# Attention scores of three row blocks in one stretch, with the smaller blocks' exponentials a step later, and two delayed steps in the SSD groups

## The chip, the cores and the metric

The kernel runs on one core of one Trainium2 chip. The metric is the time of one execution on the device in microseconds (us), as the median of several runs.

The engines that matter here: TensorE (PE in the profile) multiplies matrices and transposes tiles; PEld is its loading of weights. VectorE (DVE) and ScalarE (ACT) do elementwise work, GpSimd (POOL) a few small powers and accumulating DMAs, SyncE (SP) issues most DMAs. Results of PE land in PSUM banks of 128 x 512 fp32, of which there are eight.

## The reference

One decoder layer for 512 tokens of width 1024, all in fp32. Cut to what matters:

```python
x = x + 0.5 * swiglu(rms_norm(x, norm_ffn1_w), ffn1_w_in, ffn1_w_out)
x = x + hybrid_mixer(rms_norm(x, norm_mix_w), ...)
x = x + memory_cross_attention(rms_norm(x, norm_cross_w), rms_norm(mem, norm_mem_w), ...)
x = x + 0.5 * swiglu(rms_norm(x, norm_ffn2_w), ffn2_w_in, ffn2_w_out)
return rms_norm(x, norm_final_w)

# in hybrid_mixer: 16 SSD heads in 4 groups, and 8 heads of differential attention
logits = einsum('bqhcd,bkhcd->bhcqk', q_blk, k) * scale + bias     # c = 0, 1: two score maps
logits = where(rel <= 0, logits, -inf)                              # causal, row blocks of 128
p = softmax(logits)
w = p[:, :, 0] - lam * p[:, :, 1]
out = einsum('bhqk,bkhe->bqhe', w, v)
# each SSD group's output is gated, then normed over the group's 256 channels:
yg = yg * rsqrt(mean(yg * yg) + EPS)
```

## The kernel before

**Precision.** Nearly every matmul of weights is done three times, with both operands split into a high and a low part of type fp32r (`split_into`, lines 152 to 161: ACT copies the high part, DVE subtracts to get the low part). A projection of one 128 x 512 tile (`proj`, line 324) is 24 matmuls of 512 columns.

**Stages.** First FFN, then the mixer (attention projections, heads, SSD groups, output projections), cross-attention, second FFN. In the trace the attention heads lie between about 375 and 640 us, SSD groups 2 and 3 between about 680 and 800 us, and the second FFN starts at about 950 us.

**What sets the order.** The program is written out by an `Order` object (lines 57 to 98). It has one dense stream, of generators that are run one after the other (`od.add`, lines 1156 to 1173), and chains (`od.spawn`), each with a due time on a host clock `od.t`. Every matmul advances that clock by a rough estimate: `mm` (line 144) by (columns + 8) / 2400 for one matmul of type fp32r, that is 0.217 per 512 columns. When a chain is due it does one step; the number that it yields is the distance, on that clock and counted from the start of the step, to its next step. So a head's scores are written between the dense matmuls of the next head's projections, which yield every two matmuls.

What is written out is not yet the order on the chip. On PE, DVE and ACT a planner orders the instructions: it plays the program with estimated durations and takes, on each engine, the earliest written instruction whose operands and buffers are there by its own reckoning. `with behind(...)` (line 184) forbids it to take an instruction ahead of a given one. SP and POOL keep the written order. On the chip each engine then runs its instructions in the planned order and waits by semaphores.

**PSUM.** Two pools of four banks each: `acc` (line 130), for projections of the dense stream, and `aux` (line 133), for the chains. A tile gets a bank of its pool that is free.

**A head** (`head`, line 766) starts 3.4 (`W["h0"]`) after its keys are projected. It handles four row blocks, i = 3, 2, 1, 0, with 128 queries each and 128 (i + 1) keys. `scores` (line 770) takes two PSUM banks, one for each of the two score maps, and places the given blocks side by side in them. The contraction is over 64 rows, so that the maps' matmuls run in pairs on two halves of PE: per block three passes of one pair (high x high, high x low, low x high). Then, per block and map, DVE adds the bias and finds the minimum (line 787, output `ec` and `mn`), and ACT takes the exponential and its row sum (line 788). `combine` (line 791) joins the two maps on DVE (lines 796 to 799, the long one being `ec<-ec,rl,ec`), and `turn(j)` (line 802) transposes the j-th key block of row blocks j to 3 on PE into a bank (`pt`), from which ACT and DVE split weights `wt` for the product with the values.

The steps (lines 814 to 830), each 3.3 (`W["hs"]`) after the one before: scores of block 3; scores of block 2 and `combine(3)`; scores of blocks 1 and 0, `combine(2)` and `turn(3)`; `combine(1)`, `combine(0)` and `turn(2)`; then `turn(1)`, and `turn(0)` 2.0 later.

Head 0 runs beside `values(0)` (line 724), which holds all four `acc` banks; heads 1 to 6 run beside the projections of later heads, heads 3 and 7 partly beside the `pxbc` tiles of an SSD group. Those are read by a convolution (`conv`, line 894: one operation on ACT, three on DVE).

**An SSD group** (`group`, line 928) works on two tiles j = 0, 1. For each, ACT and DVE make decay matrices (lines 987 to 993), and after `W["gd"]` = 6.9 and an extra, PE does the products `pf` and `py` (lines 995 to 1002). After gating (lines 1016 to 1021) and a distance of 11.8 (`W["gq"]`, and 1.2 more for group 2), `sums_by_token` (line 379) sums the squares by token on PE (`nps`), copies them by DVE (`nsum`) and, 0.8 later, transposes them. `inv_rms_cols` (line 364) then takes DVE (`nv`) and a power on POOL (`ncol`), and `row_of` (line 371), after a distance of 1.5 + 1.1, spreads the result by four transpositions (`nrow`) over the partitions. DVE scales both tiles by it (line 1028) and they are split into `ysh` and `ysl`, the operands of the output projection `out_proj` (line 1128). Its first two tiles do their first six of eight inputs early and then wait for group 3's two.

Of the kernel before, what the change touches and what calls it, by code (L numbers as in the profile page):

```python
# [13 lines left out]
AF = mybir.ActivationFunctionType  # L14
ALU = mybir.AluOpType
AX = mybir.AxisListType

P = 128
T = 512
# [18 lines left out]
W = {"h0": 3.4, "hs": 3.3, "ht": 2.0, "hv": 2.08, "hp": 6.75}  # L38
# [62 lines left out]
def body(tc, a, dbg=None):  # L101
# [13 lines left out]
    def nm(s):  # L115
        uid[0] += 1
        return f"{s}_{uid[0]}"

    def s2(s, dt=F32, shape=(P, T)):
        if math.prod(shape[1:]) <= T // 2:  # L120
            return sp.tile(list(shape), dt, tag="s1", name=nm(s), bufs=NHALF)
        return sp.tile(list(shape), dt, tag="s2", name=nm(s))
# [4 lines left out]
    def small(s, n, bufs=None):  # L127
        return tiny.tile([P, n], F32, tag=s, name=nm(s), bufs=bufs)
# [4 lines left out]
    def aux(s, shape=(P, T)):  # L133
        return aux_p.tile(list(shape), F32, tag="aux", name=nm(s))
# [6 lines left out]
    V, S, G = nc.vector, nc.scalar, nc.gpsimd  # L141
    od = Order()

    def mm(out, w, x, start, stop, share=1.0):
        od.t += share * (1 if w.dtype == R32 else 4) * (x.free_size() + 8) / 2400
        newest_mm[:] = [nc.tensor.matmul(out, w, x, start=start, stop=stop).ins]  # L146
# [36 lines left out]
    @contextmanager  # L183
    def behind(ins):
        with ExitStack() as after:
            for i in ins:
                after.enter_context(tc.issue_after(i))
            yield
# [147 lines left out]
    for k in range(KT):  # L336
# [3 lines left out]
        w = s2("wa")  # L340
# [30 lines left out]
    def row_of(col, nb, apart):  # L371
        yield apart
        pr = aux("nrow", (P, nb * P))
        with behind(list(newest_mm)):
            for b in range(nb):
                transpose(pr[:, b * P : (b + 1) * P], col[:, b : b + 1].to_broadcast([P, P]))
        return pr
# [388 lines left out]
    def head(hd, q, kq, bias):  # L766
        es, w0, w1 = {}, {}, {}
        sm = [small("sm", 4) for _ in range(2)]

        def scores(*blocks):  # L770
            ps = [aux("ps") for _ in range(2)]
            parts, to = {}, 0
            for i in blocks:
                n = P * (i + 1)
                parts[i] = slice(to, to + n)
                to += n
                for j, (u, w) in enumerate(((0, 0), (0, 1), (1, 0))):
                    for c in range(2):
                        pc = slice(64 * c, 64 * c + 64)
                        mm(ps[c][:, parts[i]], q[u][pc, i * P : (i + 1) * P], kq[w][pc, :n], j == 0, j == 2)  # L780
            for i in blocks:
                n = P * (i + 1)
                es[i] = []
                for c in range(2):
                    ec = s2("ec", shape=(P, n))
                    mn = small("mn", 1, bufs=8)
                    V.tensor_tensor_reduce(out=ec[:, :n], in0=ps[c][:, parts[i]], in1=bias[:, T - n :], scale=0.125, scalar=3e38, op0=ALU.add, op1=ALU.min, accum_out=mn)  # L787
                    S.activation(ec[:, :n], ec[:, :n], AF.Exp, bias=mn, scale=-1.0, accum_out=sm[c][:, i : i + 1])  # L788
                    es[i].append(ec)

        def combine(i):

            n = P * (i + 1)
            e = es[i]
            rc = small("rc", 1)
            V.reciprocal(rc, sm[1][:, i : i + 1])
            rl = small("rl", 1)
            V.scalar_tensor_tensor(rl, sm[0][:, i : i + 1], nlam, rc, ALU.mult, ALU.mult)
            V.scalar_tensor_tensor(e[0][:, :n], e[1][:, :n], rl, e[0][:, :n], ALU.mult, ALU.add)
            e.pop()  # L800

        def turn(j):
            n = P * (4 - j)
            pt = aux("pt")
            for i in range(j, 4):
                transpose(pt[:, (i - j) * P : (i - j + 1) * P], es[i][0][:, j * P : (j + 1) * P])
            if n <= T // 2:
                both = s2("wt", R32, (P, 2, n))
                w0[j], w1[j] = both[:, 0], both[:, 1]
            else:  # L810
                w0[j], w1[j] = s2("wt", R32, (P, n)), s2("wt", R32, (P, n))
            split_into(w0[j], w1[j], pt[:, :n])

        scores(3)
        yield W["hs"]
        scores(2)
        combine(3)
        yield W["hs"]
        scores(1, 0)
        combine(2)  # L820
        turn(3)
        yield W["hs"]
        combine(1)
        combine(0)
        turn(2)
        yield W["hs"]
        turn(1)
        yield W["ht"]
        turn(0)
        yield W["hs"] + (0.8 if hd % 4 == 3 else 0.0)  # L830
        es.clear()
        while hd // 4 not in vs:
            yield 1.0
        v = vs[hd // 4]
        hs = slice((hd % 4) * P, (hd % 4 + 1) * P)
        po = aux("po")
        for n, (v_, w_) in enumerate(((0, w0), (1, w0), (0, w1))):
            for j in (0, 1, 2, 3) if n < 2 else (1, 2, 3, 0):
                mm(po[:, j * P :], v[j][v_][:, hs], w_[j], n + j == 0, n == 2 and j == 0)
        w0.clear()  # L840
        w1.clear()
        of = s2("of")
        S.activation(of, po, AF.Copy)
        yield W["hv"]
        pt = aux("ptk")
        for b in range(4):
            transpose(pt[:, b * P : (b + 1) * P], of[:, b * P : (b + 1) * P])
        ss = small("ss", 4)
        junk = s2("junk", shape=(P, P))
        for b in range(4):  # L850
            S.activation(junk, pt[:, b * P : (b + 1) * P], AF.Square, accum_out=ss[:, b : b + 1])
        ev = small("ev", 4)
        V.scalar_tensor_tensor(ev, sm[0], EPS, sm[0], ALU.mult, ALU.mult)
        V.scalar_tensor_tensor(ev, ss, 1.0 / P, ev, ALU.mult, ALU.add)
        rr = small("rr", 4)
        G.tensor_tensor(rr, ev, mhalf, ALU.pow)
        on = s2("on", shape=(P, 4, P))
        V.tensor_tensor(on, pt.rearrange("p (a b) -> p a b", b=P), rr[:, :, None].to_broadcast([P, 4, P]), ALU.mult)
        yield W["hp"]
        pt = aux("pot")  # L860
        for b in range(4):
            transpose(pt[:, b * P : (b + 1) * P], on[:, b])
        ya[hd] = split("ya", backwards(pt), wsub)
        dump(f"ya_{hd}", ya[hd][0])
# [63 lines left out]
    def group(g, bt, ct, xs, zs):  # L928
# [52 lines left out]
        for j in range(2):  # L981
            rs = rows_of.pop((g, j))
            py = aux("py")
            e2 = s2("e2")
            for hh in range(2):
                hd = 4 * g + 2 * j + hh
                pp = slice(64 * hh, 64 * hh + 64)
                r = rs[hh]
                S.activation(e2[pp], r[pp].rearrange("p a b -> p (a b)"), AF.Exp)
                for c in range(4):  # L990
                    S.activation(r[:, c], r[:, c], AF.Relu, bias=cum[:, c, hd : hd + 1], scale=-1.0)
                S.activation(r, r, AF.Exp, scale=-1.0)
                V.tensor_tensor(r, r, cbm, ALU.mult)
            yield W["gd"] + (W["gt"] if j == 0 else 0.5 if g == 2 else 0.0)
            pf = aux("pf")
            with behind(list(newest_mm)):
                for c in range(1, 4):
                    mm(pf[:, c * P : (c + 1) * P], st[c - 1][:, j * P : (j + 1) * P], ct[:, c * P : (c + 1) * P], True, True)
                for c in range(4):
                    for hh in (1, 0):  # L1000
                        pp = slice(64 * hh, 64 * hh + 64)
                        mm(py[pp, c * P : (c + 1) * P], xdt[c // 2][:, c % 2, (2 * j + hh) * 64 : (2 * j + hh + 1) * 64], rs[hh][:, c], True, True)
            if g < 3:
                decays(g + 1, j)
            dsk = dskh[:, 2 * g + j : 2 * g + j + 1]
            V.scalar_tensor_tensor(e2[:, P:], pf[:, P:], 0.5, e2[:, P:], ALU.mult, ALU.mult)
            y = s2("y")
            V.scalar_tensor_tensor(y, xs[j], dsk, py, ALU.mult, ALU.add)
            V.tensor_tensor(y[:, P:], y[:, P:], e2[:, P:], ALU.add)
            dump(f"y_{2*g+j}", y)  # L1010
            yz.append(y)
            yield W["gy"]
# [9 lines left out]
        yield W["gq"] + (1.2 if g == 2 else 0.0)  # L1022
        pn = yield from sums_by_token(sq[0], 4)
        rh = inv_rms_cols(pn, 4, 4.0 / (4 * 256), 4.0 * EPS)
        pr = yield from row_of(rh, 4, W["gn"] + 1.1)
        for j in range(2):
            n = 2 * g + j
            V.scalar_tensor_tensor(yz[j], yz[j], par[:, C_SSD + n : C_SSD + n + 1], pr, ALU.mult, ALU.mult)
# [643 lines left out]
```

## Time and profile before

| | us |
|---|---|
| median of 3 runs | 1289.73 (1289.62 to 1290.07) |
| the profiled execution's own time | 1289.51 |
| its span, first to last instruction | 1287.7 |
| PE busy in the span | 1275.9 |
| DVE busy | 969.3 |
| ACT busy | 708.2 |
| POOL busy | 111.6 |

How to read it: the span is the time in which any instruction ran; the profiled execution's time is 1.8 us longer. A timeline row gives the start in us, the length in us, engine, line of the helper that issued it (L146 for all matmuls by `mm`, L150 for transpositions), operation, output <- inputs, shapes and how many instructions were merged into the row; in brackets, the engine's idle time ahead of it and what ended that. The lengths of matmuls are modelled and overlap, so distances on PE are taken from start to start.

### The profile page before, as it was taken

The numbers are of one execution on the slowest core, as the hardware profiler recorded it, in microseconds if no ns is written. First come the engines' busy times: TensorE is split into PE (matmuls) and PEld (weight loads), VectorE is DVE, ScalarE is ACT, GpSimd is POOL, SyncE is SP. The second block draws the span as 40 slices with busy tenths as digits, with TensorE's granted clock in tenths as the row PEclk, the third lists the DMA queues.
The fourth block names the chain that finished last, engine by engine and source line by source line (L and its number), as shares of the span: only waits on it lengthen the run. The fifth ranks groups of instructions, "written<-read, shape, count | busy, mean of one in ns | idle before, by whom it ended". The sixth has DMA issues, their size and how long they took to land.

```text
span 1287.7 us, 20009 instructions
## 1 busy us (share of the span) xinstructions
PE 1275.9 (99%) x7673; PEld 1115.9 (87%) x7673; DVE 969.3 (75%) x1547; ACT 708.2 (55%) x1207; POOL 111.6 (9%) x135
## 2 busy tenths in 40 slices
PE   9999999999999999999999999999999999999996
PEld 7889998998988788877888878888899899989995
DVE  6988898788875786657768697546668878877886
ACT  7545564566654564446654566434475546545554
POOL 1001010002201011101102011020001000000000
PEclk9999999999999999999999999999999999999998
DMA  9468677789865436753376457593259776666662
GB/s 338 104 173 209 180 204 203 217 217 238 284 205 159 128 74 191 214 173 84 96 224 199 137 150 241 197 229 99 69 160 243 207 222 177 193 190 187 186 202 87
DMA packets 69695, 234.70 MB, mean 182 GB/s; under 512 B 8144, under 2 KB 9568, under 8 KB 69248
## 3 DMA queue, kind: packets, MB, share of 16 engines
q1 hardware_dynamic: 53504, 181.12, 41.9%
q0 software_dynamic: 13456, 45.67, 19.8%
q10 hardware_dynamic: 2640, 6.65, 1.6%
q8 instruction: 60, 0.98, 0.3%
q14 instruction: 35, 0.29, 0.1%
HBM read 231.25 MB, written 48.29 MB: 217 GB/s over the span
## 4 chain that ended last, share of the span: by engine, by line
PE 88%; issue 9%; ACT 1%; POOL 1%; DMA 1%; DVE 1%; POOLq 0%; DVEq 0%; ACTq 0%
PE qb L244 13%; PE pm L146 9%; PE qe L244 9%; PE qa L244 8%; PE ob L1328 7%; PE oa L1328 5%; PE oe L1328 4%; PE pk L146 3%; PE pv L146 3%; PE pq L146 3%; PE pcq L146 3%; PE pxbc L146 3%; PE pck L146 2%; PE pa L146 2%; PE pg L146 2%
## 5 line engine op out<-in xcount | busy, mean ns | idle before, releaser
L155 ACT ACTIVATE wh<-wr 128x1024 fp32r<-128x1024 f32 (+1 forms) x245 | 251.2, 1028 | 223.4 <-PE qe L244 31.0
L156 DVE TENSOR_TENSOR wl<-wr,wh 128x1024 fp32r<-128x1024 f32 (+1 forms) x245 | 290.0, 1186 | 74.6 <-ACT wh L155 60.2
L1308 ACT ACTIVATE wh<-wr 128x1024 fp32r<-128x1024 f32 (+1 forms) x74 | 72.8, 984 | 65.9 <-PE ob L1328 17.4
L1317 DVE TENSOR_TENSOR wl<-wr,wh 128x1024 fp32r<-128x1024 f32 (+1 forms) x74 | 82.7, 1126 | 12.9 <-ACT wh L1308 11.0
L788 ACT ACTIVATE ec<-ec,mn 128x512 f32<-128x512 f32 (+3 forms) x64 | 35.3, 554 | 21.9 <-DVE mn L787 21.9
L787 DVE CUSTOM_DVE_ANT_0 ec<-ps,bias 128x512 f32<-128x512 f32 (+3 forms) x64 | 28.1, 487 | 16.2 <-PE ps L146 16.1
L368 POOL TENSOR_TENSOR ncol<-nv,mhalf 128x4 f32<-128x4 f32 (+1 forms) x9 | 11.4, 1271 | 299.8 <-DVE nv L366 299.8
L901 DVE SCALAR_TENSOR_TENSOR conv<-pxbc,par,conv 128x511 f32<-128x511 f32 (+2 forms) x48 | 35.8, 745 | 1.9 <-ACT conv L897 1.3
L253 POOL DMA_DIRECT2D wr<-in_f2q x11 | 9.7, 879 | 306.1 <-DMA wr<-in_f2q 230.4
L146 PE MATMUL pxbc<-hnl,wh 128*128 128x512 f32 x128 | 35.6, 405 | 0.0
L146 PE MATMUL pxbc<-hnh,wh 128*128 128x512 f32 x128 | 34.7, 398 | 0.0
L146 PE MATMUL pxbc<-hnh,wl 128*128 128x512 f32 x128 | 32.5, 393 | 0.0
L456 DVE TENSOR_TENSOR gate<-qb,row 128x512 f32<-128x512 f32 x19 | 13.1, 692 | 20.3 <-PE qb L244 20.3
L146 PEld LDWEIGHTS pxbc<-hnh,wl 128*128 128x128 f32 x128 | 23.7, 188 | 5.2 <-issue 0.2
L146 PEld LDWEIGHTS pxbc<-hnl,wh 128*128 128x128 f32 x128 | 23.1, 188 | 4.9 <-issue 0.6
L146 PEld LDWEIGHTS pxbc<-hnh,wh 128*128 128x128 f32 x128 | 23.4, 189 | 4.6 <-issue 0.3
L253 POOL DMA_DIRECT2D wr<-in_f1q x16 | 14.0, 872 | 152.3 <-DVE wl L156 44.6
L457 ACT ACTIVATE gate<-gate 128x1024 f32<-128x1024 f32 x19 | 20.1, 1057 | 10.9 <-DVE gate L456 10.9
L146 PE MATMUL pv<-wh,hnh 128*128 128x512 f32 x64 | 25.4, 398 | 0.0
L146 PE MATMUL pv<-wh,hnl 128*128 128x512 f32 x64 | 25.1, 393 | 0.0
L155 ACT ACTIVATE s24h<-s 128x512 fp32r<-128x512 f32 x30 | 18.8, 627 | 9.0 <-DVE s L214 9.0
L155 ACT ACTIVATE s31h<-s 128x512 fp32r<-128x512 f32 x30 | 18.7, 624 | 7.3 <-DVE s L212 4.2
(472 smaller groups left out, 3506.3 us busy)
## 6 DMA issues: line engine op xcount, KB each, us to landing
wr<-in_f2q SPq DMA_DIRECT2D x44, 512.0 KB, 4.3
wr<-in_f1q SPq DMA_DIRECT2D x40, 512.0 KB, 4.7
wr<-in_f1b SPq DMA_DIRECT2D x23, 512.0 KB, 6.3
isum<-in_f2q SPq DMA_DIRECT2D x22, 512.0 KB, 6.2
wr<-isum SPq DMA_DIRECT2D x22, 512.0 KB, 3.5
wsum<-in_f2b SPq DMA_DIRECT2D x20, 512.0 KB, 5.6
wr<-wsum SPq DMA_DIRECT2D x20, 512.0 KB, 4.4
wr<-in_f1q POOLq DMA_DIRECT2D x16, 512.0 KB, 6.8
```

Source lines behind the costliest of these rows:

```text
L146: newest_mm[:] = [nc.tensor.matmul(out, w, x, start=start, stop=stop).ins]
L155: S.activation(hi, src, AF.Copy),
L156: V.tensor_tensor(lo, src, hi.bitcast(F32), ALU.subtract),
L244: newest_mm[:] = [nc.tensor.matmul(out, w_[:, wc], xs[kp][which][x_], start=first and j == 0 and f == 0 and kp == 0, stop=j == 2 and kp == ...
L253: last_sum[:] = [G.dma_start(raw, m, accum_op=ALU.add).ins]
L457: S.activation(gate, gate, AF.Silu)
L787: V.tensor_tensor_reduce(out=ec[:, :n], in0=ps[c][:, parts[i]], in1=bias[:, T - n :], scale=0.125, scalar=3e38, op0=ALU.add, op1=ALU.min, ...
L788: S.activation(ec[:, :n], ec[:, :n], AF.Exp, bias=mn, scale=-1.0, accum_out=sm[c][:, i : i + 1])
L901: V.scalar_tensor_tensor(y[:, d:], ps[:, : T - d], par[:, cw + j : cw + j + 1], y[:, d:], ALU.mult, ALU.add)
L1308: recent[:] = [S.activation(hi[:, i * n : (i + 1) * n], r, AF.Copy).ins for i, r in enumerate(raw)]
L1317: recent.append(V.tensor_tensor(lo[:, ns], r, hi[:, ns].bitcast(F32), ALU.subtract).ins)
L1328: newest_mm[:] = [nc.tensor.matmul(ps, a_[:, ts], b_[:, ws], start=first and k == 0 and j == 0, stop=k == n - 1 and j == 2, skip_group_che ...
```

## The change

Three things change.

- In heads 1 to 7, step 2 does the scores of blocks 2 and 0, side by side in two `aux` banks, and right behind them those of block 1 in two `acc` banks; then the minima of all three, the exponentials of block 2, and `combine(3)`. Step 3 has no scores left: it takes the exponentials of blocks 1 and 0, then `combine(2)` and `turn(3)` as before. Distances between steps stay. Head 0 keeps its order of scores (3, then 2, then 1 and 0); there only the exponentials of block 0 follow those of block 1 in a call of their own.
- In group 3 the products of tile j = 1 come 0.5 later, as they do in group 2 already.
- The row of a group's norm (`row_of`) comes at a distance of 1.5 + 1.4 in groups 0, 1 and 3 and of 1.5 + 4.6 in group 2, in place of 1.5 + 1.1.

```diff
-        def scores(*blocks):
-            ps = [aux("ps") for _ in range(2)]
-            parts, to = {}, 0
-            for i in blocks:
-                n = P * (i + 1)
-                parts[i] = slice(to, to + n)
-                to += n
-                for j, (u, w) in enumerate(((0, 0), (0, 1), (1, 0))):
-                    for c in range(2):
-                        pc = slice(64 * c, 64 * c + 64)
-                        mm(ps[c][:, parts[i]], q[u][pc, i * P : (i + 1) * P], kq[w][pc, :n], j == 0, j == 2)
-            for i in blocks:
+        def scores(*pairs):
+            parts = {}
+            for n_, blocks in enumerate(pairs):
+                ps, to = [(acc if n_ else aux)("ps") for _ in range(2)], 0
+                for i in blocks:
+                    n = P * (i + 1)
+                    parts[i] = [p_[:, to : to + n] for p_ in ps]
+                    to += n
+                    for j, (u, w) in enumerate(((0, 0), (0, 1), (1, 0))):
+                        for c in range(2):
+                            pc = slice(64 * c, 64 * c + 64)
+                            mm(parts[i][c], q[u][pc, i * P : (i + 1) * P], kq[w][pc, :n], j == 0, j == 2)
+            for i in parts:
                 n = P * (i + 1)
                 es[i] = []
                 for c in range(2):
                     ec = s2("ec", shape=(P, n))
                     mn = small("mn", 1, bufs=8)
-                    V.tensor_tensor_reduce(out=ec[:, :n], in0=ps[c][:, parts[i]], ..., accum_out=mn)
-                    S.activation(ec[:, :n], ec[:, :n], AF.Exp, bias=mn, scale=-1.0, accum_out=sm[c][:, i : i + 1])
-                    es[i].append(ec)
+                    V.tensor_tensor_reduce(out=ec[:, :n], in0=parts[i][c], ..., accum_out=mn)
+                    es[i].append((ec, mn))
+            exponentials(pairs[0][0])
+
+        def exponentials(*blocks):
+            for i in blocks:
+                for c, (ec, mn) in enumerate(es[i]):
+                    S.activation(ec, ec, AF.Exp, bias=mn, scale=-1.0, accum_out=sm[c][:, i : i + 1])
+                es[i] = [ec for ec, _ in es[i]]
...
-        scores(3)
+        scores((3,))
         yield W["hs"]
-        scores(2)
-        combine(3)
-        yield W["hs"]
-        scores(1, 0)
+        if hd:
+            scores((2, 0), (1,))
+            combine(3)
+            yield W["hs"]
+            exponentials(1, 0)
+        else:
+            scores((2,))
+            combine(3)
+            yield W["hs"]
+            scores((1, 0))
+            exponentials(0)
         combine(2)
         turn(3)
         yield W["hs"]
...
-            yield W["gd"] + (W["gt"] if j == 0 else 0.5 if g == 2 else 0.0)
+            yield W["gd"] + (W["gt"] if j == 0 else 0.5 if g > 1 else 0.0)
...
-        pr = yield from row_of(rh, 4, W["gn"] + 1.1)
+        pr = yield from row_of(rh, 4, W["gn"] + (1.4, 1.4, 4.6, 1.4)[g])
```

More of the change, by code (lines that the diff above doesn't have):

```diff
@@ L786, in scores @@
                     mn = small("mn", 1, bufs=8)
-                    V.tensor_tensor_reduce(out=ec[:, :n], in0=ps[c][:, parts[i]], in1=bias[:, T - n :], scale=0.125, scalar=3e38, op0=ALU.add, op1=ALU.min, accum_out=mn)
-                    S.activation(ec[:, :n], ec[:, :n], AF.Exp, bias=mn, scale=-1.0, accum_out=sm[c][:, i : i + 1])
-                    es[i].append(ec)
+                    V.tensor_tensor_reduce(out=ec[:, :n], in0=parts[i][c], in1=bias[:, T - n :], scale=0.125, scalar=3e38, op0=ALU.add, op1=ALU.min, accum_out=mn)
+                    es[i].append((ec, mn))
[5 more added lines that the diff above has]
+                es[i] = [ec for ec, _ in es[i]]
         def combine(i):
```

## The prediction

> **What bounds the kernel now.** I read the page's first part, then busy time by stage, then TensorE's waits, and last the order of instructions around the edits. The page first, then the windows (us, busy time of PE, weight loads, DVE, ACT and POOL with instruction counts, granted clock, DMA share, GB/s), then the waits of PE.
>
> ```profile
> span 1287.7 us, 20009 instructions
> PE 1275.9 (99%) x7673; PEld 1115.9 (87%) x7673; DVE 969.3 (75%) x1547; ACT 708.2 (55%) x1207; POOL 111.6 (9%) x135
> ...
> 375.00:660.00 285.00, 284.97 (x1498) 227.52 (x1497) 193.30 (x460) 152.57 (x375) 25.77 (x29) 1.00 0.51 142
> 660.00:830.00 170.00, 169.41 (x868) 137.81 (x867) 128.56 (x187) 92.72 (x159) 16.83 (x21) 1.00 0.62 188
> 830.00:1270.00 440.00, 440.00 (x2893) 403.27 (x2892) 323.12 (x447) 236.07 (x340) 25.43 (x30) 1.00 0.62 178
> ...
> PE nrow L150 <- POOL ncol L368: 0.5, 1, 0.5
> ```
>
> TensorE is the bound everywhere, at a granted clock of 1.00. The attention heads lie in the first window, the last two SSD groups in the second; behind them PE has not one free 10 ns until 1270. So a microsecond that PE saves in the first two windows reaches the end, and one that it loses does too. The busy time hides two things, since a matmul's modelled end reaches to the next start: slow starts at a change of shape, and short waits. Both must be read from start to start.
>
> **The stretch of scores that goes.** The order on PE in head 4, from its step 2 (block 2, 384 wide) to the first transposition of step 3 and on; the last two rows are a lone transposition among dense matmuls, elsewhere:
>
> ```profile
> 566.17 0.44 PE L146 MATMUL ps<-kh,qh 64*128 64x384 f32 x2
> ...
> 566.89 1.65 PE L146 MATMUL pk<-hnh,wh 128*128 128x512 f32 x6
> 568.38 1.52 PE L146 MATMUL pk<-hnl,wh 128*128 128x512 f32 x6
> 569.83 0.38 PE L146 MATMUL ps<-kh,qh 64*128 64x256 f32 x2
> 570.06 0.28 PE L146 MATMUL ps<-kl,qh 64*128 64x256 f32 x2
> 570.17 0.28 PE L146 MATMUL ps<-kh,ql 64*128 64x256 f32 x2
> ...
> 570.46 0.28 PE L146 MATMUL ps<-kh,ql 64*128 64x128 f32 x2
> 570.67 0.33 PE L150 MATMUL pt<-ident,ec 128*128 128x128 f32 x1
> 570.75 0.71 PE L146 MATMUL pk<-hnl,wh 128*128 128x512 f32 x2
> 571.30 2.00 PE L146 MATMUL pk<-hnh,wl 128*128 128x512 f32 x8
> 573.13 0.62 PE L146 MATMUL pq<-hnh,wh 128*128 128x512 f32 x2
> ...
> 790.73 0.27 PE L150 MATMUL nps<-ident,nsum 128*128 128x128 f32 x1
> 790.75 1.62 PE L146 MATMUL pm<-ysh,wl 128*128 128x512 f32 x6
> ```
>
> A dense 512-wide matmul takes 0.229 us (eight from 571.30 to 573.13). The six before the stretch take 1.45 (568.38 to 569.83) where 1.37 is due: 0.08 to enter. The first pair of 64-row matmuls takes 0.23, the next 0.11: 0.12 more. From the last pair to the transposition is 0.21, where a pair of this size takes no more than 0.11: 0.10 to leave. The transposition holds PE for 0.08 behind scores and for 0.02 among dense matmuls: 0.06. Together 0.36 per stretch, of which the last part is the least sure: **0.30 to 0.36**; I take 0.35. For heads 1 to 7 the stretch (1, 0) goes: the same 12 matmuls stand behind block 2's in one stretch, which was entered and left anyway. 7 x 0.35 = **2.45 us** (2.1 to 2.5). Head 0 keeps its three stretches; its four small exponentials only stand behind its four minima, at no price, since they feed combines two steps on.
>
> The Trainium skill, page "TensorEngine Tiling (Array Packing)", section "Key Properties", says that a change of tiling mode drains TensorE. Its one drain per change is here the 0.08 and the 0.10; by that alone the stretch would give 7 x 0.18 = 1.3 us and the forecast below would be 1288.1. The rows show the slow first pair too, and I go by them.
>
> **What moves on DVE.** The minima of blocks 0 and 1 come a step earlier. Head 4's DVE, then what matters of heads 5 (its block 2, its first transposition, its combine of block 3) and 6:
>
> ```profile
> 567.63 0.55 DVE L787 CUSTOM_DVE_ANT_0 ec<-ps,bias 128x384 f32<-128x384 f32 x1
> ...
> 569.03 0.75 DVE L799 SCALAR_TENSOR_TENSOR ec<-ec,rl,ec 128x512 f32<-128x512 f32 x1
> ...
> 570.77 0.42 DVE L787 CUSTOM_DVE_ANT_0 ec<-ps,bias 128x256 f32<-128x256 f32 x1
> ...
> 571.46 0.29 DVE L787 CUSTOM_DVE_ANT_0 ec<-ps,bias 128x128 f32<-128x128 f32 x1
> 571.67 0.29 DVE L787 CUSTOM_DVE_ANT_0 ec<-ps,bias 128x128 f32<-128x128 f32 x1
> ...
> 580.77 0.44 PE L146 MATMUL ps<-kh,qh 64*128 64x384 f32 x2
> 586.74 0.33 PE L150 MATMUL pt<-ident,ec 128*128 128x128 f32 x1
> 584.05 0.75 DVE L799 SCALAR_TENSOR_TENSOR ec<-ec,rl,ec 128x512 f32<-128x512 f32 x1
> ...
> 599.08 0.75 DVE L799 SCALAR_TENSOR_TENSOR ec<-ec,rl,ec 128x512 f32<-128x512 f32 x1
> 599.74 0.55 DVE L787 CUSTOM_DVE_ANT_0 ec<-ps,bias 128x384 f32<-128x384 f32 x1
> ```
>
> Four minima take 0.69 (570.77 to 571.46) and 0.42 (twice 0.21): 1.11 us of DVE. In heads 4 and 5 they now stand ahead of block 3's combine, which the first transposition reads (`turn(3)`). The combine would end at 569.78 + 1.11 = 570.89 in head 4 and at 584.80 + 1.11 = 585.91 in head 5. In head 6 the combine runs ahead of block 2's minima and is not touched.
>
> The transposition's written place moves forward too. A step's 3.3 is counted from the step's start, and its own scores count: (392 + 264 + 136) x 6 / 2400 = 1.98 for the three blocks, against 0.98 for one. That leaves 1.32, or four pairs of dense matmuls (0.43 each on that clock), where the rows have 12 matmuls. So it is written behind 0.72 (block 2, 566.17 to 566.89), 0.61 (blocks 1 and 0: 569.83 to 570.67, less the slow start and end) and 8 x 0.229 with 0.1 for leaving: 3.26 us behind 566.17, at **569.43**, 1.46 us before its combine ends. Head 5: 584.03, 1.88 before. Heads 1 and 2 go as 4 and 5 (the same pattern of queries and keys). Waiting in the written place would cost 2 x 1.46 + 2 x 1.88 = **6.7 us**, since every matmul of the dense stream is queued behind that transposition. Bounds: 0 to 6.7. I take 0.2, near the lower end, because the planner sets PE's order by readiness. The sums by token of group 2 show that:
>
> ```profile
> 749.85 0.43 PE L146 MATMUL nps<-ysq,ones 128*32 128x128 f32 x8
> ...
> 759.37 0.27 PE L150 MATMUL nps<-ident,nsum 128*128 128x128 f32 x1
> 759.40 1.17 PE L146 MATMUL pcv<-wh,hm 128*128 128x512 f32 x4
> 761.02 0.65 PE L150 MATMUL nrow<-ident,ncol 128*128 128x128 f32 x4 [0.45 <-POOL ncol L368]
> ...
> 780.52 1.07 PE L146 MATMUL pcv<-wh,hm 128*128 128x512 f32 x4
> 781.73 1.09 PE L146 MATMUL py<-th,xdt 128*64 128x128 f32 x16
> ```
>
> Their transposition is written 0.8 behind the sums and ran 9.5 us behind them, with dense matmuls in between: an operand that the planner reckons late costs PE nothing. What costs is its error.
>
> **Banks.** Block 1 takes two of the four accumulator banks. At step 2 of heads 1, 2, 4, 5 and 6 the other two hold the running projection and at most one that is being split, so I cost it at nothing. In head 3 a convolution still reads its bank while the third `pxbc` tile starts:
>
> ```profile
> 470.15 1.08 PE L146 MATMUL pxbc<-hnh,wh 128*128 128x512 f32 x4
> ...
> 473.08 0.74 DVE L901 SCALAR_TENSOR_TENSOR conv<-pxbc,par,conv 128x509 f32<-128x509 f32 x1
> ```
>
> If that tile had to take this very bank it would wait from 470.15 to 473.82: 3.7 us. Any freed bank will do, and the scores' two are read out with that step's minima: bounds 0 and 3.7, I take 0. The `ec` and `mn` tiles of blocks 1 and 0 are held a step longer, in pools where no row shows a wait: nothing.
>
> **The two delayed steps.** `nrow` of group 2 starts 1.62 us behind four matmuls that need 0.92 and 0.09 for following a transposition: **0.6 us** of waiting. It moves 3.5 of the host clock later, past its old place of 761.02; how far past depends on how far the planner had already put it off. Gain 0 to 0.6; I take 0.5. The other three groups' rows move by 0.3 from places without a wait: nothing. `py` of group 3 starts 1.21 behind four matmuls that need 0.92, with 0.08 for the change of shape: **0.2 us**, which the further 0.5 covers. But group 3's last row now comes 0.8 / 0.43 = two pairs of matmuls later, and the output projection waits for it:
>
> ```profile
> 793.57 0.60 PE L150 MATMUL nrow<-ident,ncol 128*128 128x128 f32 x4
> 797.21 0.61 PE L146 MATMUL pm<-ysl,wh 128*128 128x512 f32 x2
> ...
> 795.65 1.35 DVE L156 TENSOR_TENSOR ysl<-y,ysh 128x512 fp32r<-128x512 f32 x2
> ```
>
> The second low half is ready at 797.00 and used at 797.44: 0.44 to spare, against 4 x 0.229 = 0.92. Cost 0 to 0.5, less where the planner brings other matmuls forward; I take 0.1. The group's row and norm on DVE and ACT come later among the same work, and `ys` of group 2 isn't read before the output projection.
>
> **The sum.** -2.45 - 0.5 - 0.2 + 0.2 + 0.1 = -2.85 us against the profiled execution's 1289.51 (span 1287.7, 1.8 around it): 1286.66. That execution lies 0.22 below the median of 1289.73, so **1286.9**.
>
> **The rivals.**
> - *The planner puts the transposition back, but too little.* It was 0.6 early with `nrow` and 0.2 with `py`. At 0.4 in each of heads 1, 2, 4 and 5, 1.6 us come back in place of my 0.2: 1288.3. For: four chains with an operand later than the written place. Against: PE shows no such wait at any transposition of a head today.
> - *The written order holds* (the slower side). PE waits at the first transposition in heads 1, 2, 4, 5: 1289.73 - 3.15 + 6.7 = 1293.3. It decides from 5.7 us of waiting on (slower by 0.2%). Against: the 9.5 us above.
> - *The stretch doesn't stay whole*, dense matmuls coming between its parts for want of banks: only the two delays are left, 0.7: 1289.0.
> - *The delays give nothing*: `nrow` still waits 0.6 and the last row costs 0.5, `py` gains 0.2: 1289.73 - 2.45 + 0.2 + 0.5 - 0.2 = 1287.8.
> - *The convolution's bank is waited for*: 3.7 more: 1290.6.
>
> **How the numbers follow.** Forecast 0.52, with its own range 1286.3 to 1287.5; late transposition 0.20; stretch broken 0.09; idle delays 0.08; written order 0.08; bank 0.03. A measurement of this kernel can tell about 0.2%, 2.6 us, from no change: below 1287.15 is faster. Of the forecast 0.44 lies there, of the rest 0.01: faster 0.45. Slower is the written order and a worse bank, 0.09. The same: 0.46. The range must hold all but the last two cases and the lower end of the forecast: 1286.2 to 1289.2.
>
> **What the changed profile would show.** In heads 1 to 7 one `ps` stretch of 384, 128 and 256 wide pairs, some 1.33 us long, and no slow pair later. The four minima ahead of the 512-wide combine in heads 1, 2, 4 and 5. The first `pt` behind more than 8 dense matmuls there; if behind 8, a gap of 1.5 us from start to start. No POOL wait at `nrow`. The forecast is wrong if gaps over 0.3 us show ahead of `pt`, or ahead of the first `pm` that reads `ysl`, or if PE's saving is given back behind 830.

## The result: slightly slower, and the profile after

| | before | after |
|---|---|---|
| median of 12 runs, us | 1290.18 (1289.59 to 1291.35) | 1292.99 (1292.53 to 1294.14) |
| the profiled execution's own time | 1289.51 | 1292.89 |
| its span | 1287.7 | 1291.1 |

The ratio is 1.0022, with a 95% interval of 1.0014 to 1.0029: 2.8 us slower. The forecast was 1286.9 with a range of 1286.2 to 1289.2, so the time lies outside it, on the side that had been given 0.09. In the experiments below one execution of run 7 (1564.98 us) and one of run 10 (7222.68 us) stood far above the rest; the medians include them, the ratios don't.

The profile after begins so:

```profile
span 1291.1 us, 20020 instructions
...
PE 1275.2 (99%) x7673; PEld 1117.1 (87%) x7673; DVE 967.4 (75%) x1547; ACT 708.0 (55%) x1207; POOL 111.2 (9%) x135
```

The span grew by 3.4 us while PE, with the same 7673 matmuls, was busy 0.7 us less. What was added is time in which PE does nothing. The busy time by stage (window, its length, PE, weight loads, DVE, ACT, POOL, granted clock, DMA share, GB/s) says where:

```profile
375.00:660.00 285.00, 280.99 (x1487) 225.82 (x1486) 190.87 (x456) 150.02 (x366) 25.87 (x29) 1.00 0.52 141
660.00:830.00 170.00, 169.18 (x867) 137.64 (x866) 126.49 (x186) 94.63 (x166) 16.04 (x21) 1.00 0.66 190
830.00:1270.00 440.00, 440.00 (x2893) 403.40 (x2892) 323.17 (x444) 235.02 (x338) 25.44 (x30) 1.00 0.63 178
```

In the stage of the heads PE was busy for all but 0.03 of 285 us before; now 4.0 us are free. Behind 830 PE has nothing free, as before. PE's waits after (us in all, times, longest) name the instruction:

```profile
PE ptk L150 <- ACT of L857: 4.0, 4, 1.4
...
PE nrow L150 <- POOL ncol L368: 0.8, 1, 0.8
```

The first row did not exist before. `ptk` is the transposition of a head's attention output: the products with the values land in the bank `po`, ACT copies it to `of` (line 857, 843 before), and 2.08 of the host clock later (`W["hv"]`) PE transposes `of`. The four waits lie in heads 2, 3, 5 and 6, where the last products of one head fall between steps 2 and 3 of the next. Head 5's place on PE, in the timeline after:

```profile
586.78 0.85 PE L146 MATMUL po<-wt,vh 128*128 128x384 f32 x4
587.47 0.27 PE L150 MATMUL pt<-ident,ec 128*128 128x128 f32 x1
...
588.05 0.40 PE L146 MATMUL pk<-hnl,wh 128*128 128x512 f32 x1
589.40 0.66 PE L150 MATMUL ptk<-ident,of 128*128 128x128 f32 x4 [0.96 <-ACT of L857]
589.81 1.87 PE L146 MATMUL pk<-hnl,wh 128*128 128x512 f32 x7
```

From 588.05 to 589.40 one dense matmul is all that PE does, 1.35 us where 0.23 is due. The four places (heads 2, 3, 5 and 6) have 1.60, 0.97, 1.13 and 0.97 too much from start to start. Before, the scores of blocks 1 and 0 lay between the same `po` and `ptk`, and there was no wait:

```profile
585.12 0.85 PE L146 MATMUL po<-wt,vh 128*128 128x384 f32 x4
...
586.90 0.60 PE L150 MATMUL ptk<-ident,of 128*128 128x128 f32 x4
```

What ACT did meanwhile, after:

```profile
585.76 0.62 ACT L795 ACTIVATE ec<-ec,mn 128x384 f32<-128x384 f32 x1 [1.93 <-DVE mn L788]
...
587.00 0.51 ACT L795 ACTIVATE ec<-ec,mn 128x256 f32<-128x256 f32 x1
...
588.39 0.39 ACT L795 ACTIVATE ec<-ec,mn 128x128 f32<-128x128 f32 x1
...
588.77 0.57 ACT L857 ACTIVATE of<-po 128x512 f32<-128x512 f32 x1
```

And ACT in the same place before:

```profile
583.39 0.60 ACT L788 ACTIVATE ec<-ec,mn 128x384 f32<-128x384 f32 x1
...
586.01 0.60 ACT L843 ACTIVATE of<-po 128x512 f32<-128x512 f32 x1 [1.92 <-PE po L146]
587.31 0.51 ACT L788 ACTIVATE ec<-ec,mn 128x256 f32<-128x256 f32 x1 [0.70 <-DVE mn L787]
```

Before, ACT idled until `po` was there, copied it at once, and idled again until the minima of blocks 1 and 0 released their exponentials. After, those minima come right behind block 2's, so the exponentials are released ahead of the end of `po`, and the copy stands behind all six of the step (in heads 3 and 6 behind five of them). `po` ends at 587.63 by its row; `of` starts at 588.77, 1.14 us later. PE's next instruction is the transposition of it, and the whole dense stream is queued behind that. The Trainium skill, page "Perfetto Trace Analysis", section "Tensor Engine Instruction (MATMUL, LD_WEIGHTS)", says that the execution queues of ACT and DVE are strictly first in, first out; the trace agrees, since `of` had its operand 1.14 us before its turn came.

In heads 2 and 5 the six exponentials also start later: on DVE block 3's combine now goes ahead of block 2's minima (rows further down), so in head 5 the first exponential starts 3.12 us behind the first scores of step 2 (585.76 behind 582.64), where before it was 2.01 (582.78 behind 580.77). In head 6 that order on DVE is the old one, and the place has 0.97 too much all the same. What the later start adds in heads 2 and 5 was not tried by itself.

### The profile page after: what moved, and what is told of

Its sections match the earlier page's. It is cut to its first block, busy times and chain, and to the rows that moved or that the text cites. A ratio compares the mean times of both kernels' runs of the same rounds, so it can differ in the third digit from the quotient of the medians.

```text
span 1291.1 us, 20020 instructions
## 1 busy us (share of the span) xinstructions
PE 1275.2 (99%) x7673; PEld 1117.1 (87%) x7673; DVE 967.4 (75%) x1547; ACT 708.0 (55%) x1207; POOL 111.2 (9%) x135
## 4 chain that ended last, share of the span: by engine, by line
PE 85%; issue 9%; DVE 2%; ACT 2%; DMA 1%; POOL 1%; POOLq 0%; SPq 0%; DVEq 0%; ACTq 0%
PE qb L244 13%; PE pm L146 9%; PE qe L244 8%; PE qa L244 8%; PE ob L1342 7%; PE oa L1342 5%; PE oe L1342 4%; PE pv L146 3%; PE pcq L146 3%; PE pq L146 3%; PE pk L146 3%; PE pxbc L146 2%; PE pck L146 2%; PE pcv L146 2%; PE pa L146 2%
## 5 line engine op out<-in xcount | busy, mean ns | idle before, releaser
L155 ACT ACTIVATE wt<-pt 128x128 fp32r<-128x128 f32 (+3 forms) x32 | 13.8, 430 | 17.4 <-PE pt L150 17.2
```

What stands on the lines that cost most here:

```text
L155: S.activation(hi, src, AF.Copy),
```

## The experiments

The theory (A): the loss is `of` behind the exponentials, some 4.7 us of `ptk`'s waiting, and without it the change would gain. The rivals: the merged stretch itself costs (B); `ptk` is only written too close behind `po` (C); the cause is that the exponentials come "a step later" (D).

The kernel before had medians of 1290.14 to 1290.33 in the three sets of these runs, and work that no edit touches differs by more: the first `pdt` matmul on PE, behind the first FFN, starts between 374.92 and 376.89 in these profiles. So beside each ratio stands a length inside the profiled execution, from the first `pdt` matmul (374.92 before) to the first `pcq` matmul of the cross-attention (832.11 before). The heads and the SSD groups lie between the two. From that `pcq` to the end of the span all these profiles take 455.5 to 455.6, so what is lost or gained between the marks reaches the end, and a length of this size repeats to about 0.1. "Delays" are those of group 3's `py` and of the groups' rows, group 2's above all.

| kernel | `pdt` to `pcq` | against before | median | ratio to before (95%) |
|---|---|---|---|---|
| before | 457.19 | | | |
| after | 460.27 | +3.08 | 1292.99 | 1.0022 (1.0014 to 1.0029) |
| 1: exponentials behind `of` | 455.79 | -1.40 | 1289.23 | 0.9996 (0.9987 to 1.0005) |
| 2: exponentials at once | 460.01 | +2.82 | 1292.51 | 1.0019 (1.0010 to 1.0028) |
| 3: `ptk` later | 455.63 | -1.56 | 1288.17 | 0.9984 (0.9975 to 0.9993) |
| 4: heads' part only | 459.87 | +2.68 | 1293.00 | 1.0021 (1.0011 to 1.0030) |
| 5: delays only | 457.49 | +0.30 | 1290.79 | 1.0005 (0.9996 to 1.0014) |
| 6: after, row at 10.5 | 458.95 | +1.76 | 1292.20 | 1.0017 (1.0008 to 1.0026) |
| 7: 1 and 6 together | 454.55 | -2.64 | 1287.89 | 0.9980 (0.9971 to 0.9989) |
| 8: before, a stretch more per head | 460.15 | +2.96 | 1293.02 | 1.0023 (1.0013 to 1.0034) |
| 9: 3 and 6 together | 454.51 | -2.68 | 1287.44 | 0.9978 (0.9969 to 0.9986) |
| 10: before, delays with the row at 10.5 | 456.28 | -0.91 | 1289.51 | 0.9991 (0.9982 to 1.0000) |
| 11: heads' part only, exponentials behind `of` | 455.65 | -1.54 | 1288.56 | 0.9987 (0.9978 to 0.9996) |

**1. The exponentials of blocks 1 and 0 behind the copy.** The planner may not take them ahead of the newest `of`; nothing else changes.

```diff
+    newest_of = []
...
-            exponentials(1, 0)
+            with behind(list(newest_of)):
+                exponentials(1, 0)
...
-        S.activation(of, po, AF.Copy)
+        newest_of[:] = [S.activation(of, po, AF.Copy).ins]
```

> The changed kernel, with the exponentials of blocks 1 and 0 tied behind the last copy of a head's output (of) on ACT. Theory A (the new waits at ptk, 1.6, 1.0, 1.1 and 1.0 us in heads 2, 3, 5 and 6, together 4.7, come from of standing behind those exponentials in ACT's order): the waits go, one score stretch less stays, about 4.7 us below the changed kernel, 1288.3, and under the kernel before by 1.5 to 2.2. Theory B (the stretch itself costs: its banks or its early minima hold something up, and ptk is only where it shows): no more than 1 us is won, the gaps turn up at other instructions. Theory C (ptk is only written too close behind po, since the score stretch no longer lies between): waits of 0.3 us and more stay at ptk in all four heads.

It is 4.48 us shorter than the kernel after between the two marks, and PE's waits hold no `ptk` any more. The median fell less than expected: 1289.23 for 1288.3, not clearly below the kernel before. Head 5 on ACT:

```profile
585.06 0.60 ACT L859 ACTIVATE of<-po 128x512 f32<-128x512 f32 x1 [0.60 <-PE po L147]
585.56 0.50 ACT L796 ACTIVATE ec<-ec,mn 128x256 f32<-128x256 f32 x1
```

and on PE:

```profile
584.18 0.85 PE L147 MATMUL po<-wt,vh 128*128 128x384 f32 x4
...
585.44 0.40 PE L147 MATMUL pk<-hnl,wh 128*128 128x512 f32 x1
585.72 0.66 PE L151 MATMUL ptk<-ident,of 128*128 128x128 f32 x4
```

The transposition is in the same place (1.54 us behind the last `po` row's start, where the kernel after had 2.62) and has 0.05 too much in place of 1.13, since the copy goes first and four of the six exponentials follow it. With the stretch, the banks and the early minima all as in the kernel after, B falls; and C falls as the cause, since the place of `ptk` was not moved. That place is tight, though: the copy ends at 585.66 and `ptk` starts at 585.72.

**2. The exponentials at once.** All three blocks' exponentials are written in step 2.

```diff
-            exponentials(pairs[0][0])
+            exponentials(*parts)
...
-            exponentials(1, 0)
...
-            exponentials(0)
```

> The changed kernel, with the exponentials of all three blocks written in step 2, right behind their minima. Theory A: ACT takes them ahead of of as soon as the minima are there, whichever step writes them, so the four waits stay at about 4.7 us and the time at 1292.5 to 1293.3. Theory D (the exponentials' step later is what puts them in the way of of): the waits go and the time is 1288.3.

```profile
PE ptk L150 <- ACT of L855: 3.8, 4, 1.4
```

PE waits 3.8 us at `ptk`, four times, as in the kernel after (4.0), and the time is the same. The step that the change puts between minima and exponentials does nothing either way: the planner takes an exponential when its minimum is there, not where it is written. D falls. What makes the exponentials early is the minima, so the scores.

**3. `ptk` later.** The distance behind `po` grows from 2.08 to 3.88.

```diff
-W = {"h0": 3.4, "hs": 3.3, "ht": 2.0, "hv": 2.08, "hp": 6.75}
+W = {"h0": 3.4, "hs": 3.3, "ht": 2.0, "hv": 3.88, "hp": 6.75}
```

> The changed kernel, with ptk 1.8 later on the host clock (hv 3.88 in place of 2.08), ACT's order left alone. Theory A: of ends at most 1.4 us after ptk's old place, so the waits go as in e1: 1288.3, or 0.5 more if a head's last steps come late for the output projection behind heads 3 and 7. Theory B: no more than 1 us is won.

The copy still comes behind the exponentials, now without harm. On ACT and on PE, head 5:

```profile
586.40 0.39 ACT L795 ACTIVATE ec<-ec,mn 128x128 f32<-128x128 f32 x1
...
586.79 0.57 ACT L857 ACTIVATE of<-po 128x512 f32<-128x512 f32 x1
```

```profile
584.79 0.85 PE L146 MATMUL po<-wt,vh 128*128 128x384 f32 x4
...
586.06 1.99 PE L146 MATMUL pk<-hnl,wh 128*128 128x512 f32 x8
587.88 0.60 PE L150 MATMUL ptk<-ident,of 128*128 128x128 f32 x4
```

Eight matmuls of `pk<-hnl,wh` stand where one stood, and `of` is there when PE comes to it. So the late copy has a price only because the distance of 2.08 had been set for an early copy. Either end can be mended: the place of the copy or the place of its reader.

**4 and 5. The two parts alone.** Run 4 undoes the delays in the kernel after; run 5 makes only them in the kernel before.

```diff
-            yield W["gd"] + (W["gt"] if j == 0 else 0.5 if g > 1 else 0.0)
+            yield W["gd"] + (W["gt"] if j == 0 else 0.5 if g == 2 else 0.0)
...
-        pr = yield from row_of(rh, 4, W["gn"] + (1.4, 1.4, 4.6, 1.4)[g])
+        pr = yield from row_of(rh, 4, W["gn"] + 1.1)
```

> The changed kernel without its two delays in the SSD groups: heads alone. Theory A: the waits at ptk stay (4.7 us); nrow of group 2 waits 0.6 as before in place of 0.95, py of group 3 0.2 in place of 0.1: 0.1 to 0.3 us below the changed kernel, 1292.7. If the delays were the loss, the time would be 1290 or less.

> The kernel before with the two delays of the change alone (py of group 3 and the rows of the SSD groups). Prediction's step: 0.5 + 0.2 - 0.1 = 0.6 us below the kernel before. Theory A, from the kernel with the heads' part alone, where the waits were as before: the transposition of group 2's row (nrow) waits some 0.95 us from start to start in place of 0.61, py's excess goes from 0.30 to 0.21, and the time is 0.2 to 0.4 us ABOVE the kernel before, which this comparison calls no change. Attention heads as before: no wait of ptk on ACT.

The heads' part alone loses 2.68, the delays alone 0.30; together 2.98, against 3.08 for the whole. The delays were to gain 0.6 and cost a little. The row of group 2 in the kernel after:

```profile
762.57 0.27 PE L150 MATMUL nps<-ident,nsum 128*128 128x128 f32 x1
762.60 0.94 PE L146 MATMUL pm<-yah,wl 128*128 128x512 f32 x3
764.32 0.65 PE L150 MATMUL nrow<-ident,ncol 128*128 128x128 f32 x4 [0.79 <-POOL ncol L368]
```

The row still comes as early as its operand allows, now behind three matmuls in place of four, and waits 0.95 from start to start in place of 0.61. The planner had put it off beyond its written place already. An estimate from rows of before, with the host clock taken as us and the sums by token as run where they were written: they start at 749.85, the transposition is written 0.8 behind them and the row 2.6 behind that, at 753.3, while it ran at 761.02. With 3.5 more it is written at 756.8, still ahead of the planned place, and such a written place delays nothing. Why one matmul fewer was put in front isn't shown.

**6. The row later still.** Its distance in the kernel after is 10.5 in place of 4.6, behind the place that the planner chose (762.7 by the same estimate).

```diff
-        pr = yield from row_of(rh, 4, W["gn"] + (1.4, 1.4, 4.6, 1.4)[g])
+        pr = yield from row_of(rh, 4, W["gn"] + (1.4, 1.4, 10.5, 1.4)[g])
```

> The changed kernel with the delay of group 2's row 10.5 in place of 4.6, so that its written place lies behind the place where the planner put it, not ahead. Theory (the row was moved too little): the wait of nrow on POOL (0.95 us of start to start) is gone, the waits of ptk on ACT (some 4.7 us) stay, and the time is some 0.9 us below the changed kernel. Rival (the wait goes with the row, whatever its place, or the output projection waits for it later): nrow still waits, or a wait of the same size shows ahead of the first pm that reads ysl, and the time is that of the changed kernel.

```profile
764.89 1.55 PE L146 MATMUL pcv<-wh,hm 128*128 128x512 f32 x6
766.28 0.85 PE L146 MATMUL pcv<-wl,hm 128*128 128x512 f32 x3
766.96 0.61 PE L146 MATMUL pcv<-wh,hm 128*128 128x512 f32 x2
767.41 0.60 PE L150 MATMUL nrow<-ident,ncol 128*128 128x128 f32 x4
```

In this timeline eleven more dense matmuls go first and no wait is left. The length falls by 1.32, more than the 0.9 expected. Beside the 0.95 at `nrow`, 0.1 goes at `py` and 0.2 ahead of group 3's last `pf` (in the kernel after the six dense matmuls from 776.80 take 1.55, where 1.37 is due); the last 0.1 was not traced. No new wait shows at the output projection.

**7, 9 and 10. Both mended, and the delays mended alone.** Run 7 is run 1 with the row at 10.5, run 9 is run 3 with it, run 10 is run 5 with it; no other edits.

> The changed kernel with the exponentials of blocks 1 and 0 held behind the last copy of po (as in the run where ptk no longer waited) and the row of group 2 at 10.5. If the two losses are independent: that run's 1289.23 less some 0.9, so about 1288.3, below the kernel before by 1.5 to 2.2 us; no wait of ptk on ACT, none of nrow on POOL. If the row's wait only moves: 1289.2.

> The changed kernel with ptk written 1.8 later behind po (hv 3.88, the edit that gave 1288.17) and the row of group 2 at 10.5 (which removed 1.17 us of nrow's wait and py's excess in the run where the row alone was moved). If the two mends are independent of how ptk's wait is removed: 1288.17 less some 1.0 to 1.2, so 1287.0 to 1287.3, at or below the kernel with both mended by holding the exponentials (1287.89). If they are not: 1288.2.

> The kernel before with the two delays alone, the row of group 2 at 10.5 in place of 4.6. Theory: what the prediction wanted of the delays comes when the written place lies behind the planner's: nrow's 0.61 and py's 0.2 are gone, 0.6 to 0.9 us between the first pdt and the first pcq on TensorE (457.19 before), and the time 0.6 to 0.9 below the kernel before. Rival: the gain of the row's move exists only with the changed heads: no more than 0.2.

The row's move is worth the same wherever it is made: 1.32 (after to 6), 1.24 (1 to 7), 1.12 (3 to 9), 1.21 (5 to 10). So is the mend of `ptk`: 4.48 (after to 1), 4.64 (after to 3), 4.40 (6 to 7), 4.44 (6 to 9), and by the next run 4.22 (4 to 11). So the two losses add up, to within 0.2 or 0.4 us. Run 9 has the lowest median of the study, 0.2% below the kernel before, though a little above the 1287.0 to 1287.3 that were expected and not clearly below run 7. Its page and its waits of PE, which hold nothing but the start:

```profile
span 1285.4 us, 20017 instructions
...
PE 1274.3 (99%) x7673; PEld 1117.3 (87%) x7673; DVE 966.4 (75%) x1547; ACT 707.3 (55%) x1207; POOL 113.5 (9%) x135
```

```profile
PE init L355 <- DVE ones_r L351: 1.4, 1, 1.4
```

Run 10's time is too near to the kernel before to tell by itself; its length is 0.91 less, and the two waits that are gone from its PE (0.61 at `nrow`, 0.2 at `py`) make up 0.8 of it.

**8. One stretch more.** In the kernel before, block 0's scores are written behind the first transposition of step 3, so each head enters and leaves the 64-row shape once more with the same matmuls.

```diff
-        scores(1, 0)
+        scores(1, 0, between=lambda: turn(3))
         combine(2)
-        turn(3)
```

Inside `scores`, `between()` is called ahead of its second block.

> The kernel before with the scores of block 0 written behind the first transposition of step 3, so that every head has one stretch of scores more: the same matmuls, one change into the 64-row shape and one out of it more per head. If the gain of merging is the slow starts (prediction 0.35 per stretch; 0.24 by the runs so far): 8 x 0.24 to 0.35, so 1.9 to 2.8 us more than the kernel before between the first pdt and the first pcq on TensorE, and about that much in the time. Rival (merging gains by something else, as the earlier minima): at most 0.5 us more.

```profile
572.65 0.38 PE L146 MATMUL ps<-kh,qh 64*128 64x256 f32 x2
...
573.20 0.33 PE L150 MATMUL pt<-ident,ec 128*128 128x128 f32 x1
573.46 0.33 PE L146 MATMUL ps<-kh,qh 64*128 64x128 f32 x2
...
573.94 0.73 PE L146 MATMUL pk<-hnl,wh 128*128 128x512 f32 x2
```

In head 4, from the 256-wide scores to the next dense matmul, 1.29 us go by where the kernel before took 0.92 (569.83 to 570.75): 0.37 for one stretch, and 2.96 / 8 = 0.37 over all heads. Half of it is the transposition, which between scores holds PE for 0.26 (573.20 to 573.46) and behind them took 0.08. The other half is a second end of a stretch (0.09 more from the last 256-wide pair to the next row) and a second slow first pair (0.16 where it took 0.06). So slow starts are a real price of the shape, and an added one costs a little more than the 0.35 predicted.

**11. The merging alone.** The heads' part without the delays, with run 1's edit.

> The heads' part of the change alone (no delays), with the exponentials of blocks 1 and 0 held behind the last copy of po. So the merging by itself, with nrow and py as before. By rows of head 4 (1.72 us for two stretches before, 1.43 for the merged one) 0.29 per head: 7 x 0.29 = 2.0 us less between the first pdt and the first pcq on TensorE, 455.2, and the time 1.6 to 2.0 below the kernel before. Prediction's step: 2.45 (454.7). Rival (the merge gives less than its stretches by a cost elsewhere in the heads): 1.0 or less.

1.54 less than before, with `nrow` and `py` as before. The same edit against a partner with the same delays gives 1.70 (run 5 to run 1) and 1.73 (10 to 7); with `ptk` written later in place of the tie it is 1.86 (5 to 3) and 1.77 (10 to 9). So the merging gives 1.54 to 1.86, 0.22 to 0.27 per head. The heads differ: from the block 3 scores of one head to those of the next, with the same matmuls between, run 11 takes 0.22 less than before in head 1, 0.31 in head 4 and 0.27 in head 6, but only 0.12 in head 2 and 0.06 in head 5.

## Why the prediction was wrong

It put the sum at -2.85; the length between the marks changed by +3.08. By its own steps:

**The moved exponentials: the step that failed.** The prediction costed the order on DVE and PE for the earlier minima, and wrote "at no price" for head 0's exponentials, but for heads 1 to 7 it named no price at all for ACT: a term put at nothing without a reason. It did not ask what else is queued on ACT between the old and the new place of six exponentials. There stands `of`, whose reader is on PE a fixed 2.08 behind. It cost 4.2 to 4.6 us by the five pairs above, some three quarters of the whole miss of 5.9. Without it the change gains: run 1 is 1.40 shorter than before. Its row was there to be read: before, `of` at 586.01 started in the middle of an idle stretch that only the late minima kept open.

**The slower rival** had the right side and nearly the right time (1293.3), but by luck, since its mechanism was another: a late first transposition in heads 1, 2, 4 and 5. It is refuted. The four minima were to stand ahead of block 3's combine on DVE; they do not. Heads 4 and 5 after, on DVE:

```profile
570.25 0.75 DVE L806 SCALAR_TENSOR_TENSOR ec<-ec,rl,ec 128x512 f32<-128x512 f32 x1
570.92 0.55 DVE L788 CUSTOM_DVE_ANT_0 ec<-ps,bias 128x384 f32<-128x384 f32 x1
...
584.50 0.75 DVE L806 SCALAR_TENSOR_TENSOR ec<-ec,rl,ec 128x512 f32<-128x512 f32 x1
585.17 0.55 DVE L788 CUSTOM_DVE_ANT_0 ec<-ps,bias 128x384 f32<-128x384 f32 x1
```

The combine goes first even of block 2's minima, and in head 4 the first `pt` stands behind eight dense matmuls, as it was written, without the gap of 1.5 that was to be there. Why the planner now puts the combine first isn't shown. The 0.2 and the bound of 6.7 were both for a thing that didn't happen; the argument that the planner goes by readiness held, and was not carried over to ACT, where the same rule does the harm. There too readiness in the planner's reckoning seems to have decided, since the step in which the exponentials are written made no difference (run 2).

**The stretch.** Its mechanism is right, its size too large: 0.35 per head predicted, 0.22 to 0.27 measured, 2.45 against 1.54 to 1.86 in all. Head 4 on PE after:

```profile
568.35 0.44 PE L146 MATMUL ps<-kh,qh 64*128 64x384 f32 x2
...
568.97 0.23 PE L146 MATMUL ps<-kh,qh 64*128 64x128 f32 x2
...
569.26 0.34 PE L146 MATMUL ps<-kh,qh 64*128 64x256 f32 x2
569.43 0.28 PE L146 MATMUL ps<-kl,qh 64*128 64x256 f32 x2
569.55 0.28 PE L146 MATMUL ps<-kh,ql 64*128 64x256 f32 x2
569.76 1.66 PE L146 MATMUL pk<-hnh,wh 128*128 128x512 f32 x6
...
571.72 0.27 PE L150 MATMUL pt<-ident,ec 128*128 128x128 f32 x1
571.74 1.62 PE L146 MATMUL pk<-hnl,wh 128*128 128x512 f32 x6
```

The stretch is one, as said, and takes 1.41 (568.35 to 569.76), where 1.33 was expected; with 0.02 for the transposition 1.43. Before, the same work took 0.72, 0.92 and 0.08 to enter: 1.72. So 0.29 is saved here. Of the 0.36 of the prediction 0.05 comes back inside: the first pair of block 1, in the other banks, takes 0.17 (569.26 to 569.43), the next 0.12. The mean over the heads is lower because of heads 2 and 5 (run 11); what takes the rest there isn't settled. The Trainium skill, page "TensorEngine Tiling (Array Packing)", section "Key Properties", says that a change of tiling mode drains TensorE. With the 0.18 per stretch that the prediction read from the rows, that alone would have given 1.3; the runs lie between this and the rows' 2.45, nearer to the 1.3, and for the added stretch of run 8 (0.37) above both.

**Banks.** None of PE's waits after is for a bank, the convolution's or another: cost 0, as taken.

**The delays.** Predicted -0.5 - 0.2 + 0.1; measured +0.30. The step "it moves 3.5 of the host clock later, past its old place" failed: the move was shorter than what the planner had put it off by, a doubt that the prediction had named and then set aside. The gain existed (0.91 in run 10) and needed 10.5. `py`'s 0.2 was right in kind but came whole only with the row: from the last `pf` to `py`, 0.2 us more than its matmuls and changes of shape need before, 0.1 after, nothing in runs 6, 7, 9 and 10. No wait shows ahead of the first `pm` that reads `ysl`, so the 0.1 was nothing.

**The sum again**, with what was measured: -1.6 for the merging, +0.3 for the delays, +4.4 for `of`: +3.1, against the +3.08 of the marks and +2.8 of the medians. The terms are differences of the same lengths, so that they add up proves little; that each comes out alike wherever it is measured says more. What the prediction said would show it wrong, gaps ahead of `pt` or ahead of `pm`, or a gain given back behind 830, did not show; the gap was in a place that it had not listed.

## What to carry to other kernels

When an operation is made ready earlier, list what stands between its old and its new place on every engine it leads to, not only on the one that bounds: on ACT, which took its queue in order, three or four exponentials in each of four heads, released ahead of a copy of 0.6 us, cost some 4.4 us in all because that copy was awaited. A fixed distance between a producer and its reader holds only for the order it was set for, so look for the tight ones (here 2.08) whenever work is moved past them. And before a step is delayed to cover a wait, find out where the planner already puts it; here a written place ahead of that gained nothing and cost 0.3 us, while one behind it gained 0.9 over the kernel before.

## What was not expected of the hardware

A lone fp32 transposition between two stretches of 64-row matmuls keeps PE for 0.26 us until the next pair starts (run 8, 573.20 to 573.46), where among dense 512-wide matmuls it takes 0.02 (571.72 to 571.74): the added stretch cost 0.37 per head where a merged one gave back 0.22 to 0.27. And within one stretch of the same shape the first pair in other banks took 0.17 in place of 0.12; that the banks are its cause was not tried.
